# Where the down-projection's gate is applied: on the input matrix ahead of time, or on row sums and two weights inside the stage

## The chip, the cores and the metric

The kernel runs on one core of one Trainium2 chip. The metric is the device time of one execution in microseconds, lower is better; the median of three runs is compared. Engines are called as the profile calls them: PE is the matrix engine (TensorE), DVE the vector engine, ACT the scalar engine, POOL GpSimd, and SP the engine whose queue issues nearly all DMA transfers. SBUF is the on-chip memory, PSUM the accumulators of PE.

## The reference, cut to what matters

One layer of a diffusion backbone on 2048 latent tokens of width 1024, with 256 context tokens in front: RMSNorm and modulation, one input projection for a gated recurrence (HGRN2) and a spatial gating unit, an output projection, then a gated MLP with a 3x3 convolution, and a last RMSNorm. The change concerns only the end:

```python
x = x + g1 * (o @ w_out[l])
h2 = modulate(rmsnorm(x, norm_ffn[l]), sh2, sc2)
x = x + g2 * conv_ffn(h2, w_up[l], conv_w[l], conv_b[l], w_down[l], rows)
return rmsnorm(x, norm_final)
# conv_ffn ends in: return (a * gelu(gc)) @ w_down        (2048 x 2816) @ (2816 x 1024)
```

`g2` is one number for each of the 1024 output columns, computed from the input `c`. Multiplying the product's columns by g2, or the columns of `w_down` by g2 before the product, is the same in exact arithmetic.

## The kernel before

**Precision.** Products are made in three passes on PE: each fp32 operand is split into a high part (a cast on ACT, `split`, line 131) and a low part (a subtraction), and `mm3` adds high x high, high x low and low x high. A split on DVE's `Kept` wrapper shows as line 80.

**Phase one** (the first 1150 us): adaLN vectors, input projection, recurrence and gating units. Work that is not urgent is fed in by a "pump", `bg_q`, which at fixed points of the matmul order lets a generator take one more step. After the blocks that compute the adaLN rows (among them `g_d[1]`, which is g2) come `w_out_ops`, `conv_taps` and `w_down_ops`. The last one loads `w_down` in 22 pieces of 128 x 2 x 512, multiplies each by g2 on DVE (line 970) and stores it to the DRAM tiles `wd_d`.

**The up-projection** (about 1150 to 2019 us) is a fast matrix product with seven products in place of eight; it writes the activations `m_d` to DRAM.

**The down-projection** (2019 us to the end) is one, too. The rows of the result are taken in two halves of 1024, its columns in two halves of 512, and the inner dimension of 2816 in 11 pairs of 128-wide blocks j. There are seven rounds q = 0 to 6. In each round one combination of quarters of the activations is multiplied by one combination of quarters of the weights, for all 11 pairs: 77 steps, n = 11 q + j. A step is 8 row groups x 3 passes = 24 matmuls of 512 columns into the 8 PSUM banks, one bank for each row group i. At the end of a round each bank is emptied (`evict`) and the results go on being added up in the SBUF tiles `odd[i]` and `even[i]` (128 x 2 x 512 each: rows of the second and of the first half, two column halves). What can wait is put in the list `side`, from which one function is taken in each later step (`sums_behind`).

Per step, `load(n + 3)` fetches operands, `prepare(n + 2)` makes the combinations and splits them, and the 24 matmuls of step n follow. In `prepare`, `a` is the activations' operand (into the tile `mhl`), `b` the weights' (into `thl`); both have three buffers. Where a combination is used again it is kept in `sS` and `sT` (`S_`, `T_` for the pair j). Tiles for loads go round: four of `mr` (activations, and rows of x later), five of `wr` inside `sT` (weights). DVE's instructions in this stage are pinned to program order; those of POOL and ACT may be moved by the scheduler that lays out each engine's queue when the kernel is built.

Before the change the rows of x after the first residual (`xn_d`) come in twice: rows of the first half are loaded into `even` in round 0, so that round 1's `evict` adds onto them; rows of the second half are loaded in the steps of round 5 and added in `odd_rows`, two steps later. The last round's results are normed and written out (`odd_sum`, `odd_out`), those of the first half in round 6 (`square`, `root`, `row_out`).

Of the kernel before, what the change touches and what calls it, by code (L numbers as in the profile page):

```python
# [9 lines left out]
F32 = mybir.dt.float32  # L10
# [8 lines left out]
P = 128  # L19
D = 1024  # L20
# [28 lines left out]
def view(t, off, dims):  # L49

    return bass.AP(t.tensor, t.offset + off, [list(t.ap[0])] + [list(d) for d in dims])
# [32 lines left out]
def tile_trunk(ctx, tc, x, c, cx, c_ctx, w_ada, b_ada, norm_mix, norm_ffn, w_in, hg_norm, sgu_g, sgu_b,  # L84
# [30 lines left out]
    xh_d = dr.tile([P, NK, TH], F32, name="xh_d")  # L115
    xl_d = dr.tile([P, NK, TH], F32, name="xl_d")
    wo_d = dr.tile([P, NK, 2, D], F32, name="wo_d")
    wd_d = [dr.tile([P, 2, D], F32, name=f"wd{j}") for j in range(NF // 2)]
    xn_d = [dr.tile([P, D], F32, name=f"xn{i}") for i in range(2 * NCH)]

    def rstd(pool, ss, n, scale, bias=EPS, keep=lambda i: i, out=None):
# [67 lines left out]
    with es1:  # L189
# [16 lines left out]
        def raw_tile():  # L206
            return p1.tile([P, D], F32, tag="raw", name="raw", bufs=3)
# [749 lines left out]
                    st(wo_d[:, k, 1, cl], g)  # L957
                    yield 2.5

        def w_down_ops():  # L960

            for n in range(2):
                cl = slice(n * 512, n * 512 + 512)
                g = pm.tile([P, 512], F32, tag="acc", name="g2")
                ld(g, g_d[1:2, cl].broadcast_to([P, 512]))
                for j in range(NF // 2):
                    raw = raw_tile().rearrange("p (a c) -> p a c", a=2)
                    ld(raw, w_down[2 * j * P:2 * (j + 1) * P, cl].rearrange("(a p) c -> p a c", p=P))
                    yield 9.0
                    pin(V.tensor_mul(raw, raw, view(g, 0, [[0, 2], [1, 512]])))  # L970
                    st(wd_d[j][:, :, cl], raw)
                    yield 2.5

        def silu(dst, scale):
            def f(n0, n, pj):
                t = pm.tile([P, 512], F32, tag="sig", name="sig", bufs=2)
# [4 lines left out]
        def head(hh, h):  # L981

            prev = (hh, h - 1) if h else (hh - 1, NH - 1)
            before = (hh, h - 2) if h > 1 else (hh - 1, NH - 2 + h)
            t = {}

            def pre_v():
                if before[0] >= 0:
                    need(hg_q, (before[0], before[1], "end"))
                    if any(g["key"] == before for g in gates):  # L990
                        gates_done()
                t["sgt"] = ph.tile([P, TH], F32, tag="sgt", name="sgt", bufs=2)
                t["vt"] = ph.tile([P, TH], F32, tag="vt", name="vt", bufs=2)

            def pre_q():
                if prev[0] >= 0:
                    need(hg_q, (prev[0], prev[1], "diag"))
                t["qs"] = ph.tile([P, TH], F32, tag="qs", name="qs")

            def pre_g():  # L1000
                if prev[0] >= 0:
                    need(hg_q, (prev[0], prev[1], "keys"))
                else:
                    need(bg_q, "x1")
                    for e in range(8):
                        bg_q.add(ada_block(e))
                    bg_q.add(w_out_ops())
                    bg_q.add(conv_taps())
                    bg_q.add(w_down_ops())
                t["F"] = pk.tile([P, 2, TH], F32, tag="F", name="F", align_bytes=AL)  # L1010
                t["K"] = pk.tile([P, 2, TH], F32, tag="K", name="K", bufs=2, align_bytes=AL)

            def post():
                hg_q.add(marked(hg(hh, h, t["F"], t["K"], t["qs"], t["vt"], t["sgt"]), (hh, h, "end")))
                if hh == 1:
                    hg_q.add(deferred(h))
            front = tile_banks(4 * HW + h * P, lambda: silu(t["sgt"], 1.0), TH, pre_v)
            front += tile_banks(2 * HW + h * P, lambda: sink_v(t["vt"]))
            front += tile_banks(3 * HW + h * P, lambda: silu(t["qs"], float(P) ** -0.5), TH, pre_q)
            ff = tile_banks(0 * HW + h * P, lambda: sink_gate_x(t["F"], t["K"], 1, 0), TH, pre_g)  # L1020
            fb = tile_banks(1 * HW + h * P, lambda: sink_gate_x(t["F"], t["K"], 0, 1))
            return front, [ff[0], fb[0], ff[1], fb[1]], post
# [464 lines left out]
        return m_d[2 * j + c][:, r * TH:(r + 1) * TH]  # L1487

    def b_src(c, n, j):
        return wd_d[j][:, c, n * 512:(n + 1) * 512]  # L1490

    ops = {}

    def cast(n, a, b, at, bt):

        split(*at, a, V)
        split(*bt, b, V)
        ops[n] = *at, *bt
# [81 lines left out]
    odd = [pd_.tile([P, 2, 512], F32, name=f"odd{i}") for i in range(NCH)]  # L1580
    even = [pd_.tile([P, 2, 512], F32, name=f"even{i}") for i in range(NCH)]
    nf = pd_.tile([P, D], F32, name="nf")
    nw = [0]
    ra, rb = {}, {}

# [11 lines left out]
    def get(t, src):  # L1597
        pin(ld(t, src))
        return t
# [37 lines left out]
    def prepare(n):  # L1637

        if n >= 7 * NJ:
            return  # L1640
        q, j = divmod(n, NJ)
        (a, b), (a2_, b2) = ra.pop(n), rb.pop(n, (None, None))
        if q == 4:
            V.tensor_sub(a, a, a2_)
            V.tensor_sub(b, b, b2)
        cast(n, a, b, slot_s(n), slot_t(n))
        S_, T_ = sS[:, j, :], sTj(j)
        if q == 1:
            V.tensor_add(S_, a2_, S_)
            V.tensor_sub(T_, b2, T_)  # L1650
        elif q == 2:
            V.tensor_sub(S_, S_, a2_)
            V.tensor_sub(T_, b2, T_)
        elif q == 3:
            V.tensor_sub(S_, a2_, S_)
        elif q == 5:
            V.tensor_sub(T_, T_, b2)

    def square(t, ss):
        jk = pd_.tile([P, D], BF16, tag="jk", name="jk")  # L1660
# [2 lines left out]
    def flat(t):  # L1663
        return t.rearrange("p a b -> p (a b)")
# [12 lines left out]

    xts, odd_ss = {}, {}

    def odd_rows(i):  # L1680

        o = odd[i]
        V.tensor_add(flat(o), flat(o), xts.pop(i))
        odd_ss[i] = pd_.tile([P, 2], F32, name=f"oss{i}")
        square(o[:, 1, :], odd_ss[i][:, 1:2])
        V.tensor_scalar(out=odd_ss[i][:, 1:2], in0=odd_ss[i][:, 1:2], scalar1=D * EPS, scalar2=None, op0=ALU.add)
        if i == NCH - 1:
            V.tensor_mul(o[:, 1, :], o[:, 1, :], nf[:, 512:])
# [22 lines left out]
    def sums_behind(q, i):  # L1711
        o, e = odd[i], even[i]
        if q == 1:
            side.append(lambda: V.tensor_add(e[:, 0, :], e[:, 0, :], o[:, 0, :]))
        elif q == 3:
            def f():
                V.tensor_add(e[:, 1, :], e[:, 1, :], o[:, 0, :])
                V.tensor_add(e[:, 1, :], e[:, 1, :], o[:, 1, :])
            side.append(f)
        elif q == 4:  # L1720
            def f():
                V.tensor_add(o[:, 1, :], o[:, 1, :], o[:, 0, :])
                xts[i] = get(mr(), xn_d[NCH + i])
                if i > 1:
                    odd_rows(i - 2)
            side.append(f)
            if i == NCH - 1:
                side.extend([lambda: odd_rows(i - 1), lambda: odd_rows(i)])
        elif q == 5:
            def f():  # L1730
                ss = pd_.tile([P, 2], F32, tag="ss", name="ss", bufs=4)
                square(flat(e), ss[:, 0:1])
                row_out(i, flat(e), root(ss[:, 0:1]))
            side.append(f)

    def evict(q, i, pd):
        o, e = odd[i], even[i]
        if q in (0, 2):
            S.copy(o[:, q // 2, :], pd)
        elif q in (1, 5):  # L1740
            V.tensor_add(e[:, q // 5, :], pd, e[:, q // 5, :])
        elif q in (3, 4):
            V.tensor_add(o[:, 0, :], pd, o[:, 0, :])
        sums_behind(q, i)
# [9 lines left out]
    for n in range(3, 7 * NJ - NB):  # L1754
        q, j = divmod(n, NJ)
        if j == 0:
            pds = banks()
        if n in range(4, 4 + NCH):
            ld(flat(even[n - 4]), xn_d[n - 4])
        if n == 2 * NJ - 3:  # L1760
            ld(nf, norm_final.rearrange("(o d) -> o d", o=1).broadcast_to([P, D]))
            S.mul(nf, nf, float(D) ** 0.5)
        if n == 6 * NJ:
            tail = pd_.tile([P, NJ * TH], F32R, tag="sS", name="tail", align_bytes=AL)
            tail_s = tail[:, :8 * TH].rearrange("p (s w c) -> p s w c", s=4, w=2)
        if q < 6:
            load(n + 3)
            prepare(n + 2)
        else:
            for k in ((2,), (3,), (4,), (5,), (6, 7), (8, 9), (10,))[j]:  # L1770
                prepare(6 * NJ + k)
            for k in ((3,), (4,), (5, 6), (7, 8), (9, 10), (), ())[j]:
                load(6 * NJ + k)
        for i in range(NCH):
            down(pds[i], n, i, j == 0, j == NJ - 1)
            if j == NJ - 1:
                evict(q, i, pds[i])
        for _ in range(1 + (q == 6)):
            if side and j < NJ - 1:
                side.pop(0)()  # L1780
# [29 lines left out]
```

## Time and profile before

| | us |
|---|---|
| runs of the kernel before | 2452.80, 2452.89, 2457.57 |
| their median | 2452.89 |
| the profiled execution | 2449.13 |
| its span on the core | 2447.3 |
| PE busy in it | 2408.3 |
| DVE busy | 1785.5 |
| ACT busy | 943.7 |
| POOL busy | 873.4 |

The granted clock of PE was 0.998 over the profiled execution. In the profile's rows an instruction stands as line, engine, operation, output<-inputs by the program's names, sizes as partitions x elements, and count. In a timeline the first number is the start in us from the span's start and the second the duration; in brackets stands how long the engine was idle before it, and on whom it waited. A row of the windows has the window, its length, then the busy time (and number) of PE, PEld (loading of weights into PE), DVE, ACT and POOL, PE's granted clock, the share of DMA in use and GB/s. A row of waits has who waited on whom, the sum in us, how often, and the longest. A row of a line's or tile's instructions has the shortest, median and longest duration in ns.

### The profile page before, as it was taken

The page shows a single profiled execution, that of the slowest core. Times are in us where ns is not written, and L with a number is a line of the kernel's source. Part 1 is how long each engine was busy: PE and PEld are TensorE (multiplying, and loading weights), DVE is VectorE, ACT ScalarE, POOL GpSimd, SP SyncE. Part 2 cuts the span into 40 slices and gives each one's busy share as a digit, 9 for nine tenths or more (in the row PEclk, how much of TensorE's full clock was granted, in tenths as well). Part 3 has the DMA queues.
Part 4 walks back from the last instruction along what each step waited for, and adds up shares of the span by engine and source line. Part 5 has one row for each costly group of instructions (what it writes and reads, how often), then busy time and mean ns, then how long its engine had stood idle before and what let it go on. Part 6 is the DMA issues. An engine that isn't in the chain of part 4 may idle for free.

```text
span 2447.3 us, 32836 instructions
## 1 busy us (share of the span) xinstructions
PE 2408.3 (98%) x11859; PEld 2000.8 (82%) x11859; DVE 1785.5 (73%) x2445; ACT 943.7 (39%) x1614; POOL 873.4 (36%) x795
## 2 busy tenths in 40 slices
PE   7999999999999999999999999999999999999998
PEld 4788888888888888788788888878888888888887
DVE  5867685756776776466698877769999992776875
ACT  4554334333344433354443333333333342332343
POOL 1232010110111122001688778787778870000002
PEclk9999999999999999999999999999999999999999
DMA  8365446564254234668822222562222238934645
GB/s 310 109 210 171 141 136 209 193 225 147 96 185 155 87 104 149 233 216 261 297 86 88 82 96 83 177 237 85 86 93 94 83 102 349 318 125 146 228 151 197
DMA packets 307855, 400.13 MB, mean 163 GB/s; under 512 B 33113, under 2 KB 216161, under 8 KB 304621
## 3 DMA queue, kind: packets, MB, share of 16 engines
q1 hardware_dynamic: 304404, 397.28, 48.1%
q8 instruction: 94, 1.54, 0.3%
q10 hardware_dynamic: 3289, 0.76, 0.1%
q14 instruction: 68, 0.56, 0.1%
HBM read 288.85 MB, written 109.13 MB: 163 GB/s over the span
## 4 chain that ended last, share of the span: by engine, by line
PE 40%; DVE 7%; issue 3%; POOL 2%; ACT 1%; DMA 0%; SPq 0%; POOLq 0%; ACTq 0%; DVEq 0%
PE up L65 25%; PE dn L65 15%; DVE dn L1377 3%; DVE edges L1382 1%; DVE gp L1458 1%; ACT dn L1374 1%; POOL Al L132 0%; POOL ra L1669 0%; POOL rr L1670 0%; DVE keep L1452 0%; POOL raw L1195 0%; DVE keep L1468 0%; ACT cv L1396 0%; ACT Ah L131 0%; POOL cv L1469 0%
## 5 line engine op out<-in xcount | busy, mean ns | idle before, releaser
L1377 DVE SCALAR_TENSOR_TENSOR dn<-gp,taps,dn 128x1024 f32<-128x1024 f32 x352 | 448.3, 1280 | 21.4 <-ACT dn L1374 18.1
L65 PE MATMUL up<-yf,Ah 128*128 128x512 f32 x1232 | 393.7, 389 | 0.0
L65 PE MATMUL dn<-thl,mhl 128*128 128x512 f32 x1680 | 381.5, 389 | 1.2 <-ACT thl L131 1.2
L132 POOL TENSOR_TENSOR Al<-raw,Ah 128x512 fp32r<-128x512 f32 x264 | 342.9, 1307 | 92.0 <-ACT Ah L131 79.0
L65 PEld LDWEIGHTS dn<-thl,mhl 128*128 128x128 f32 x1680 | 315.0, 188 | 67.7 <-ACT thl L131 2.0
L65 PE MATMUL pj<-xh,whi 128*128 128x512 f32 x896 | 363.1, 406 | 0.0
L65 PE MATMUL pj<-xh,wlo 128*128 128x512 f32 x896 | 350.6, 392 | 2.0 <-DVE wlo L132 2.0
L65 PE MATMUL pj<-xl,whi 128*128 128x512 f32 x896 | 351.4, 392 | 1.1 <-POOL xl L132 1.0
L65 PE MATMUL up<-xah,Al 128*128 128x512 f32 x704 | 275.6, 392 | 3.8 <-POOL Al L132 3.8
L65 PE MATMUL up<-xah,Ah 128*128 128x512 f32 x704 | 274.5, 390 | 0.6 <-ACT Ah L131 0.6
L65 PEld LDWEIGHTS up<-yf,Ah 128*128 128x128 f32 x1232 | 231.2, 188 | 48.1
L131 ACT CAST Ah<-raw 128x512 fp32r<-128x512 f32 x264 | 160.5, 618 | 278.4 <-PE up L65 208.4
L65 PE MATMUL up<-xal,Ah 128*128 128x512 f32 x528 | 205.5, 389 | 0.0
L65 PE MATMUL up<-yf,Al 128*128 128x512 f32 x528 | 205.2, 389 | 0.0
L65 PEld LDWEIGHTS pj<-xh,wlo 128*128 128x128 f32 x896 | 168.3, 188 | 38.2 <-DVE wlo L132 2.7
L65 PEld LDWEIGHTS pj<-xh,whi 128*128 128x128 f32 x896 | 168.6, 188 | 33.3 <-issue 3.5
L65 PEld LDWEIGHTS pj<-xl,whi 128*128 128x128 f32 x896 | 168.8, 188 | 32.2 <-POOL xl L132 1.9
L65 PE MATMUL dn<-wo,o 128*128 128x512 f32 x768 | 182.9, 394 | 2.1 <-ACT o L131 1.6
L580 POOL TENSOR_TENSOR K<-K,tot 128x512 f32<-128x512 f32 x40 | 50.0, 1251 | 343.9 <-PE sc L65 194.5
L65 PEld LDWEIGHTS dn<-wo,o 128*128 128x128 f32 x768 | 141.9, 188 | 31.8 <-ACT o L131 2.0
L65 PEld LDWEIGHTS up<-xah,Al 128*128 128x128 f32 x704 | 132.1, 188 | 36.5 <-POOL Al L132 9.4
L65 PEld LDWEIGHTS up<-xah,Ah 128*128 128x128 f32 x704 | 132.2, 188 | 28.0 <-ACT Ah L131 1.0
(315 smaller groups left out, 3923.7 us busy)
## 6 DMA issues: line engine op xcount, KB each, us to landing
raw<-in_w_up_dram SPq DMA_DIRECT2D x88, 512.0 KB, 4.7
mr<-m SPq DMA_DIRECT2D x85, 512.0 KB, 5.0
raw<-in_w_in_dram SPq DMA_DIRECT2D x68, 512.0 KB, 4.2
sT<-wd SPq DMA_DIRECT2D x88, 256.0 KB, 4.1
raw<-in_w_ada_dram SPq DMA_DIRECT2D x32, 512.0 KB, 3.8
yf<-yd SPq DMA_DIRECT2D x14, 1024.0 KB
m<-cv SPq DMA_DIRECT2D x22, 544.0 KB, 2.7
raw<-in_w_down_dram SPq DMA_DIRECT2D x22, 512.0 KB, 4.3
```

Of the source, the lines that this page charges most:

```text
L65: return self.engine.matmul(out, lhsT, rhs, **kw)
L131: keep(S.copy(hi, raw))
L132: (eng or G).tensor_sub(lo, raw, hi.bitcast(F32))
L580: e.tensor_mul(view(K2, row * W + o, src), view(K, o, src), view(tot, t0, [[4, n], [ts, 2], [0, B]]))
L1374: S.activation(cr, gt[:, 0:RH, 0:GW], AF.Identity, bias=cvb[:, f:f + 1], scale=taps[:, f:f + 1])
L1377: V.scalar_tensor_tensor(out=cr, in0=gt[:, t // 3:t // 3 + RH, t % 3:t % 3 + GW], scalar=taps[:, t * NF + f:t * NF + f + 1], in1=cr, op0=A ...
L1382: V.scalar_tensor_tensor(out=e[:, 0, :], in0=gt[:, 1, t % 3:t % 3 + GW], scalar=taps[:, t * NF + f:t * NF + f + 1], in1=e[:, 0, :], op0=AL ...
L1458: V.tensor_add(g_rows(hh, f + c, n2), quad(p, kind), quad(add, kind))
```

## The change

The gated copy of `w_down` is no longer made: `w_down_ops` and the tiles `wd_d` are removed, and the down-projection loads the same pieces from the input `w_down`. The gate is applied inside the stage, on POOL (`G`):

- In round 5 each prepared weight `b` is multiplied by the second column half of g2 before its cast, and the kept combination `T_`, which round 6 uses, by the first half, after its subtraction. These are 22 multiplications of 128 x 512. The results of rounds 5 and 6 come out gated.
- `even[i]` is multiplied by g2 as a whole behind round 3, and `odd[i]` behind round 4: 16 multiplications of 128 x 1024, run from `side` in the first eight steps of rounds 4 and 5.
- Since the sums are ungated until then, the rows of x are added later, for both halves, in `rows_x`, one step behind the multiplication of `odd[i]`. Both row blocks are loaded in round 5. Round 1's results are copied into `even` by ACT instead of added by DVE; behind round 3 one addition takes the place of two.
- A tile `g2` (128 x 1024) is loaded once at the start of the stage.

```diff
--- before.py
+++ after.py
@@ -115,7 +115,6 @@
     xh_d = dr.tile([P, NK, TH], F32, name="xh_d")
     xl_d = dr.tile([P, NK, TH], F32, name="xl_d")
     wo_d = dr.tile([P, NK, 2, D], F32, name="wo_d")
-    wd_d = [dr.tile([P, 2, D], F32, name=f"wd{j}") for j in range(NF // 2)]
     xn_d = [dr.tile([P, D], F32, name=f"xn{i}") for i in range(2 * NCH)]
 
     def rstd(pool, ss, n, scale, bias=EPS, keep=lambda i: i, out=None):
@@ -957,20 +956,6 @@
                     st(wo_d[:, k, 1, cl], g)
                     yield 2.5
 
-        def w_down_ops():
-
-            for n in range(2):
-                cl = slice(n * 512, n * 512 + 512)
-                g = pm.tile([P, 512], F32, tag="acc", name="g2")
-                ld(g, g_d[1:2, cl].broadcast_to([P, 512]))
-                for j in range(NF // 2):
-                    raw = raw_tile().rearrange("p (a c) -> p a c", a=2)
-                    ld(raw, w_down[2 * j * P:2 * (j + 1) * P, cl].rearrange("(a p) c -> p a c", p=P))
-                    yield 9.0
-                    pin(V.tensor_mul(raw, raw, view(g, 0, [[0, 2], [1, 512]])))
-                    st(wd_d[j][:, :, cl], raw)
-                    yield 2.5
-
         def silu(dst, scale):
             def f(n0, n, pj):
                 t = pm.tile([P, 512], F32, tag="sig", name="sig", bufs=2)
@@ -1006,7 +991,6 @@
                         bg_q.add(ada_block(e))
                     bg_q.add(w_out_ops())
                     bg_q.add(conv_taps())
-                    bg_q.add(w_down_ops())
                 t["F"] = pk.tile([P, 2, TH], F32, tag="F", name="F", align_bytes=AL)
                 t["K"] = pk.tile([P, 2, TH], F32, tag="K", name="K", bufs=2, align_bytes=AL)
 
@@ -1487,7 +1471,7 @@
         return m_d[2 * j + c][:, r * TH:(r + 1) * TH]
 
     def b_src(c, n, j):
-        return wd_d[j][:, c, n * 512:(n + 1) * 512]
+        return w_down[(2 * j + c) * P:(2 * j + c + 1) * P, n * 512:(n + 1) * 512]
 
     ops = {}
 
@@ -1580,6 +1564,8 @@
     odd = [pd_.tile([P, 2, 512], F32, name=f"odd{i}") for i in range(NCH)]
     even = [pd_.tile([P, 2, 512], F32, name=f"even{i}") for i in range(NCH)]
     nf = pd_.tile([P, D], F32, name="nf")
+    g2 = pd_.tile([P, D], F32, name="g2")
+    ld(g2, g_d[1:2, :].broadcast_to([P, D]))
     nw = [0]
     ra, rb = {}, {}
 
@@ -1643,6 +1629,8 @@
         if q == 4:
             V.tensor_sub(a, a, a2_)
             V.tensor_sub(b, b, b2)
+        if q == 5:
+            G.tensor_mul(b, b, g2[:, 512:])
         cast(n, a, b, slot_s(n), slot_t(n))
         S_, T_ = sS[:, j, :], sTj(j)
         if q == 1:
@@ -1655,6 +1643,7 @@
             V.tensor_sub(S_, a2_, S_)
         elif q == 5:
             V.tensor_sub(T_, T_, b2)
+            G.tensor_mul(T_, T_, g2[:, :512])
 
     def square(t, ss):
         jk = pd_.tile([P, D], BF16, tag="jk", name="jk")
@@ -1677,10 +1666,11 @@
 
     xts, odd_ss = {}, {}
 
-    def odd_rows(i):
-
-        o = odd[i]
-        V.tensor_add(flat(o), flat(o), xts.pop(i))
+    def rows_x(i):
+
+        o, (xo, xe) = odd[i], xts.pop(i)
+        V.tensor_add(flat(even[i]), flat(even[i]), xe)
+        V.tensor_add(flat(o), flat(o), xo)
         odd_ss[i] = pd_.tile([P, 2], F32, name=f"oss{i}")
         square(o[:, 1, :], odd_ss[i][:, 1:2])
         V.tensor_scalar(out=odd_ss[i][:, 1:2], in0=odd_ss[i][:, 1:2], scalar1=D * EPS, scalar2=None, op0=ALU.add)
@@ -1714,18 +1704,19 @@
             side.append(lambda: V.tensor_add(e[:, 0, :], e[:, 0, :], o[:, 0, :]))
         elif q == 3:
             def f():
-                V.tensor_add(e[:, 1, :], e[:, 1, :], o[:, 0, :])
-                V.tensor_add(e[:, 1, :], e[:, 1, :], o[:, 1, :])
+                V.tensor_add(e[:, 1, :], o[:, 0, :], o[:, 1, :])
+                G.tensor_mul(flat(e), flat(e), g2)
             side.append(f)
         elif q == 4:
             def f():
                 V.tensor_add(o[:, 1, :], o[:, 1, :], o[:, 0, :])
-                xts[i] = get(mr(), xn_d[NCH + i])
-                if i > 1:
-                    odd_rows(i - 2)
+                G.tensor_mul(flat(o), flat(o), g2)
+                xts[i] = get(mr(), xn_d[NCH + i]), get(mr(), xn_d[i])
+                if i:
+                    rows_x(i - 1)
             side.append(f)
             if i == NCH - 1:
-                side.extend([lambda: odd_rows(i - 1), lambda: odd_rows(i)])
+                side.append(lambda: rows_x(i))
         elif q == 5:
             def f():
                 ss = pd_.tile([P, 2], F32, tag="ss", name="ss", bufs=4)
@@ -1737,8 +1728,10 @@
         o, e = odd[i], even[i]
         if q in (0, 2):
             S.copy(o[:, q // 2, :], pd)
-        elif q in (1, 5):
-            V.tensor_add(e[:, q // 5, :], pd, e[:, q // 5, :])
+        elif q == 1:
+            S.copy(e[:, 0, :], pd)
+        elif q == 5:
+            V.tensor_add(e[:, 1, :], pd, e[:, 1, :])
         elif q in (3, 4):
             V.tensor_add(o[:, 0, :], pd, o[:, 0, :])
         sums_behind(q, i)
@@ -1755,8 +1748,6 @@
         q, j = divmod(n, NJ)
         if j == 0:
             pds = banks()
-        if n in range(4, 4 + NCH):
-            ld(flat(even[n - 4]), xn_d[n - 4])
         if n == 2 * NJ - 3:
             ld(nf, norm_final.rearrange("(o d) -> o d", o=1).broadcast_to([P, D]))
             S.mul(nf, nf, float(D) ** 0.5)
```

## The prediction

> **What bounds the kernel now.** I read the page, the windows, the waits, and last the timeline of each engine in the last stage.
>
> ```profile
> span 2447.3 us, 32836 instructions
> PE 2408.3 (98%) x11859; PEld 2000.8 (82%) x11859; DVE 1785.5 (73%) x2445; ACT 943.7 (39%) x1614; POOL 873.4 (36%) x795
> ```
>
> PE is busy for 98% of the span, so the time changes only where PE is made to wait, or stops waiting. The change touches two places: phase one, where `w_down_ops` runs, and the down-projection at the end.
>
> ```profile
> L970 DVE TENSOR_TENSOR raw<-raw,g x22: 1209/1216/2310, 546.4 to 821.2; 128x1024 f32<-128x1024 f32 x22
> ...
> 546.00:824.00 278.00, 277.95 (x1619) 242.89 (x1618) 192.87 (x274) 107.70 (x223) 36.54 (x37) 1.00 0.43 146
> ...
> PE dn L65 <- ACT thl L131: 1.2, 2, 0.7
> POOL ra L1669 <- ACT jk L1661: 359.2, 3, 357.3
> ```
>
> The first row is the 22 gating multiplications in phase one; the second is the window in which they lie (length, then PE, PEld, DVE, ACT, POOL busy). PE is busy for 277.95 of 278.00 us there. The third row is all that PE waits for in the down-projection between 2036 and 2440 us: 1.2 us. The fourth shows POOL without work there: it stands idle for 357.3 us in one piece.
>
> So PE bounds the down-projection too, and the question is how far ahead of PE the splits of its operands run. A step is one of 77 products (7 rounds q of 11); call the flat number n. ACT casts step n+2 when PE ends step n-1, since three buffers go round:
>
> ```profile
> 2254.93 1.05 ACT L131 CAST mhl<-mr 128x1024 fp32r<-128x1024 f32 x1 [3.87 <-PE dn L65]
> ...
> 2320.17 1.06 ACT L131 CAST mhl<-sS 128x1024 fp32r<-128x1024 f32 x1 [3.82 <-PE dn L65]
> ...
> 2347.37 1.05 ACT L131 CAST mhl<-sS 128x1024 fp32r<-128x1024 f32 x1 [3.20 <-PE dn L65]
> ...
> 2352.81 1.05 ACT L131 CAST mhl<-sS 128x1024 fp32r<-128x1024 f32 x1 [3.25 <-PE dn L65]
> ```
>
> PE starts n=43 at 2254.93 and n=55 (first of round 5) at 2320.17; the step is 2352.81-2347.37 = 5.44 us. VectorE (DVE) in round 4, then its adds at the round's end, then one step of round 5, then the adds that end round 5:
>
> ```profile
> 2266.09 0.68 DVE L80 TENSOR_TENSOR thl<-sT,thl 128x512 fp32r<-128x512 f32 x1
> 2266.69 1.41 DVE L80 TENSOR_TENSOR even<-even,odd 128x512 f32<-128x512 f32 x2
> 2268.02 1.22 DVE L80 TENSOR_TENSOR mr<-mr 128x1024 f32<-128x1024 f32 x1
> 2269.16 0.68 DVE L80 TENSOR_TENSOR sT<-sT 128x512 f32<-128x512 f32 x1
> 2270.44 1.23 DVE L80 TENSOR_TENSOR mhl<-mr,mhl 128x1024 fp32r<-128x1024 f32 x1 [0.59 <-ACT mhl L131]
> ...
> 2318.21 4.87 DVE L80 TENSOR_TENSOR odd<-dn,odd 128x512 f32<-128x512 f32 x8
> ...
> 2324.73 0.68 DVE L80 TENSOR_TENSOR sT<-sT 128x512 f32<-128x512 f32 x1
> ...
> 2349.14 1.21 DVE L80 TENSOR_TENSOR mhl<-sS,mhl 128x1024 fp32r<-128x1024 f32 x1
> 2350.28 0.69 DVE L80 TENSOR_TENSOR thl<-sT,thl 128x512 fp32r<-128x512 f32 x1
> 2350.88 0.68 DVE L80 TENSOR_TENSOR sT<-sT 128x512 f32<-128x512 f32 x1
> 2351.48 0.69 DVE L80 TENSOR_TENSOR odd<-odd 128x512 f32<-128x512 f32 x1
> 2352.08 1.22 DVE L80 TENSOR_TENSOR odd<-odd,mr 128x1024 f32<-128x1024 f32 x1
> 2354.51 0.15 DVE L80 TENSOR_SCALAR oss<-oss 128x1 f32<-128x1 f32 x1 [1.21 <-ACT jk L1661]
> 2354.58 1.22 DVE L80 TENSOR_TENSOR mhl<-sS,mhl 128x1024 fp32r<-128x1024 f32 x1
> ...
> 2377.40 4.87 DVE L80 TENSOR_TENSOR even<-dn,even 128x512 f32<-128x512 f32 x8
> ```
>
> From start to start, an operation on 128x1024 takes DVE 1.14 us (2349.14 to 2350.28) and one on 128x512 takes 0.60. DVE's queue keeps program order, and it is nearly full: in round 5 the step takes 2354.58-2349.14 = 5.44 us, 1.21 of it idle for ACT's square. The weights of n=46 are split at 2266.69; PE starts n=46 at 2254.93+3x5.44 = 2271.25, so the lead in round 4 is 4.5 us. That is all the cover there is.
>
> **The change part by part. Phase one:** 22 multiplications (27 us of DVE by 1.216 each), 22 loads and 22 stores of 512 KB leave, and two broadcasts. PE idles 0.05 us in that window, so this removes nothing from the end: 0, at most 0.05. Reading `w_down` instead of the copy changes an address, not a count or a size: 0.
>
> **Rounds 0 to 3.** Eight loads of x rows move from round 0 to round 5, and one broadcast of g2, 512 KB, is put at the head of SP's queue, with the first loads of the stage behind it.
>
> ```profile
> mr<-m SPq DMA_DIRECT2D x85, 512.0 KB, 5.0
> ...
> L1739 ACT COPY odd<-dn x16: 580/592/648, 2076.6 to 2201.5; 128x512 f32<-128x512 f32 x16
> ```
>
> A load of 512 KB lands 5.0 us after its issue; the ends are -1.2 (all of PE's wait gone) and +5.0 (one landing more in front of everything). I take 0, since loads run three steps, 16 us, ahead of PE. Round 1's eight results are copied by ACT, where DVE added them before; the 16 copies of rounds 0 and 2 are done so already, at 592 ns each under PE's 0.68 per bank (5.44/8): 0.
>
> **What POOL gets.** Eight multiplications of 128x1024 (`e` by g2) in round 4's first eight steps; eight more (`o` by g2) in round 5's first eight; and in each of round 5's eleven prepares two of 128x512 (`b`, `T_`), two steps ahead. Prices, and what POOL and DVE do to each other:
>
> ```profile
> 1598.62 1.28 POOL L132 TENSOR_TENSOR Al<-raw,Ah 128x512 fp32r<-128x512 f32 x1
> 1599.88 1.28 POOL L1469 TENSOR_TENSOR cv<-keep,cv 128x512 f32<-128x512 f32 x1
> ...
> 751.65 1.83 POOL L675 TENSOR_TENSOR nt<-nt,gu 128x512 f32<-128x512 f32 x1 [6.67 <-ACT gu L680]
> ...
> 751.11 1.23 DVE L132 TENSOR_TENSOR wlo<-raw,whi 128x1024 fp32r<-128x1024 f32 x1 [2.43 <-ACT whi L131]
> 752.25 2.31 DVE L970 TENSOR_TENSOR raw<-raw,g 128x1024 f32<-128x1024 f32 x1
> ...
> L1382 DVE SCALAR_TENSOR_TENSOR edges<-gp,taps,edges x66: 270/1076/1392, 1608.8 to 1984.8; 128x64 f32<-128x64 f32 x66
> ...
> L1458 DVE TENSOR_TENSOR gp<-up,keep x88: 675/684/694, 1180.1 to 1977.1; 128x512 f32<-128x512 f32 x88
> ...
> 1220.00:1980.00 760.00, 756.71 (x3328) 623.40 (x3327) 655.53 (x715) 279.41 (x442) 609.69 (x518) 1.00 0.32 107
> ```
>
> POOL does 128x512 every 1.26 us, say 1.25; the trace has no 128x1024 of it, which I take as two halves, 2.5 (an estimate). The rows about 751 us are the heart of this forecast. POOL's multiplication took 1.83 instead of 1.28: it stood until DVE's subtraction was through at about 752.25. DVE's next operation took 2.31 instead of 1.216: POOL's ended at 753.48, and DVE's 1.08 us later. They ran one after the other, not together. The last rows say which operations this hits. POOL is busy for 610 of 760 us there; `edges`, with both inputs in SBUF, is stretched from 270 ns to a median of 1076, while `gp<-up,keep`, which reads one input from PSUM, stays at 675 to 694. In the down-projection every split, add and subtraction of DVE but the adds at a round's end has both inputs in SBUF. So POOL's time must be added to DVE's.
>
> The Trainium skill, SBUF — State Buffer, section Who interferes with whom, states this as an exclusive lock: a DVE instruction with two SBUF inputs and a GpSimd one that reads SBUF never overlap, and issue order decides who stands. The trace agrees (2.31 = 1.23 + 1.08); without the lock the time would be the first rival's. The Trainium skill, GPSIMD Engine Reference, section 3.1, gives 4497 ns for 2048 fp32 columns; halved (an estimate) that is 2.25 for 128x1024 and would lower the sum by 16x0.25 = 4 us.
>
> **Round 4.** DVE per step: two of 1.14, three of 0.60 (the second `even` add is removed) = 4.08; with POOL's 2.5 it is 6.58, 1.14 over the step. Eight such steps: 9.1 less the lead of 4.5 = 4.6 us late at n=54. Then POOL's `b` for n=55 (1.25) and DVE's two splits (1.74) end 2.99 us after PE starts n=54; the step to n=56 is 4.84 (2.34 of DVE, 2.5 of POOL); then the subtraction of `T_` 0.60 and the first add that frees a bank 0.60: 9.03, where PE is through at 5.44. PE waits 3.6 us more; in the trace of before that add began 2 us ahead of it. **Late by 8.2 at n=55.**
>
> **Round 5.** The eight adds read PSUM, so POOL's queue runs beside them for nothing. They end 4.2 us after PE resumes at n=55, the splits of n=57 at 5.9, and PE needs those at 10.9: 4.94 ahead. The next step costs 2.34+0.60 of DVE and 5.0 of POOL = 7.94: 2.44 ahead. Then come seven steps (splits of n=59 to 65) with `rows_x`, which adds both row blocks (2x1.14, one more than before): 2.34+0.60+2.28+5.0 = 10.22, 4.78 over each. 7x4.78-2.44 = 31.0. DVE's wait for ACT's square lies under POOL's work. Splits of n=66: 6.47, 1.0 over. Before round 5's adds DVE splits n=67 (1.74) and does one add (0.60): PE waits 2.3. **Late by 8.2+31.0+1.0+2.3 = 42.5 at n=66.** Behind that POOL has only the small root operations it had, and round 6 runs as before.
>
> **Sum.** The profiled execution took 2449.13 us; 2449.1+42.5 = 2491.6. The median of the runs, 2452.89, lies 3.8 above it; on that scale 2495. Ends: by 1.08, 0.54, 1.23 and 2.46 as what an operation holds (752.25 to the end of the row), the same count gives 35; with the 1.21 us idle of DVE exposed in seven steps it is 51.
>
> **Rivals.** (1) Not slower: no standing for each other in this stage. POOL's 5.0 per step fit in 5.44. DVE's own line in round 5 becomes 2.34+0.60+2.28 and 0.9 to 1.2 of waiting, some 6.2; eight steps use 8x0.76 = 6.1 of the 6.3 us by which n=57 is ahead (2320.17+10.88, less 2324.73 where its splits have ended), and PE waits up to 1 us: 2454. It decides if both engines' operations keep 1.22 and 1.25 us side by side; the rows at 751 us speak against it. (2) POOL's queue order alone, without the standing: the subtraction of `T_`, then 1.25+2.5+1.25 on POOL, a cast of 0.6, two of 0.60: 6.8 and some 0.2 of signals (an estimate), 7.0 per step; 1.56 over in eight, 12.5, less the lead of 6.3, and a little at the rounds' ends: 7 us, 2460. It needs `b` to stand behind `o` in POOL's queue. (3) Worse: ACT's squares, or a queue order that leaves the shared path idle between them, add over 1.5 us to each of 16 steps: 2519. (4) Faster by the relief of phase one: 5 us would be wanted where PE idles 0.05.
>
> **How the numbers follow.** Forecast 0.76, rival 1 0.09, rival 2 0.05, rival 3 0.08, rival 4 0.02. The likeliest gives 2495. Its bounds 35 and 51 are 2488 and 2504; below I also allow that round 4's multiplications find gaps (-8.2) and that rounds' ends cost nothing (-3.3), down to 2476; above some of rival 3, to 2510. Rivals 1, 2 and 4 stay out. A measurement of this kernel tells 0.2%, 4.9 us, from no change: faster 0.02, same 0.09, slower 0.89.
>
> **What would show it.** DVE's 128x1024 operations in rounds 4 and 5 with a mean well over 1.22 us and single ones near 2.3 or 3.6; POOL's of 128x1024 at 2.5 or more; PE waits on `thl`/`mhl` of 40 us in all, none before n=50, most between n=59 and 65 in pieces of 4 to 5 us; phase one with PE as busy as now. I am wrong if the step of round 5 stays under 7 us, or if PE waits elsewhere, for a load of w_down or x.

## The result, and the profile after

The changed kernel takes 2490.08 us (median of four runs, 2488.14 to 2492.80) against 2452.85 for the kernel before (four runs): 37.2 us more, ratio 1.015 with a 95% interval of 1.0132 to 1.0168. The profiled execution took 2490.86 us.

The page of the changed kernel, its span and its engines:

```profile
span 2489.1 us, 32763 instructions
PE 2424.7 (97%) x11859; PEld 2011.4 (81%) x11859; DVE 1809.5 (73%) x2415; ACT 947.1 (38%) x1622; POOL 965.1 (39%) x833
```

The number of matmuls is the same, 11859, so the two traces can be laid side by side matmul by matmul. At the start of round 4 the changed kernel's are 4.7 us late, at the first of round 5 (n=55) 10.8, at n=67 42.0, and nothing is added behind that. From round 4 to the first step of round 6 the change therefore costs 6.1 + 31.2 = 37.3 us; the 4.7 from earlier stages lies within what profiles of kernels with the same earlier stages differ by (below).

The windows of the changed kernel, for the stretch in which the 22 gating multiplications lay in phase one, and for the 100 us around round 5 (columns as in the table's note above: PE, PEld, DVE, ACT, POOL, clock, DMA share, GB/s):

```profile
546.00:824.00 278.00, 277.94 (x1612) 242.61 (x1611) 168.85 (x252) 108.41 (x225) 36.14 (x38) 1.00 0.20 65
2320.00:2420.00 100.00, 78.25 (x293) 60.64 (x291) 93.27 (x82) 27.37 (x46) 65.71 (x30) 0.90 0.47 155
```

In phase one DVE lost 24 us of work and the DMA share fell from 0.43 to 0.20, while PE's busy time went from 277.95 to 277.94: the relief bought nothing. In round 5 the picture is turned over: DVE is busy for 93 of 100 us and PE for 78. What PE waits for in the down-projection, from the waits (the cast of a split is line 130 in this kernel):

```profile
PE dn L65 <- DVE thl L80: 17.7, 9, 3.8
PE dn L65 <- DVE even L80: 4.2, 1, 4.2
PE dn L65 <- ACT thl L130: 1.6, 2, 0.9
```

PE's own timeline shows when:

```profile
2249.63 59.32 PE L65 MATMUL dn<-thl,mhl 128*128 128x512 f32 x261
2309.24 5.78 PE L65 MATMUL dn<-thl,mhl 128*128 128x512 f32 x24 [0.29 <-DVE thl L80]
2315.52 5.52 PE L65 MATMUL dn<-thl,mhl 128*128 128x512 f32 x23 [0.51 <-DVE thl L80]
...
2323.98 34.98 PE L65 MATMUL dn<-thl,mhl 128*128 128x512 f32 x144 [1.59 <-DVE thl L80]
2362.81 7.31 PE L65 MATMUL dn<-thl,mhl 128*128 128x512 f32 x24 [3.84 <-DVE thl L80]
2372.39 7.34 PE L65 MATMUL dn<-thl,mhl 128*128 128x512 f32 x24 [2.27 <-DVE thl L80]
2381.97 7.36 PE L65 MATMUL dn<-thl,mhl 128*128 128x512 f32 x24 [2.23 <-DVE thl L80]
2391.53 5.73 PE L65 MATMUL dn<-thl,mhl 128*128 128x512 f32 x24 [2.21 <-DVE thl L80]
2401.10 8.56 PE L65 MATMUL dn<-thl,mhl 128*128 128x512 f32 x24 [3.84 <-DVE thl L80]
...
2420.32 10.04 PE L65 MATMUL dn<-thl,mhl 128*128 128x512 f32 x36 [4.19 <-DVE even L80]
```

Until 2309 us there is no gap: the lead absorbs the first steps of round 4. Small gaps follow in its last steps, then none for 35 us, and from 2362.81 on PE starts a step each 9.58 us in place of 5.44, behind the split of `thl`. The last row is the wait for round 5's first addition. Now DVE, in two steps of round 4 and in one of round 5:

```profile
2278.28 1.21 DVE L80 TENSOR_TENSOR mr<-mr 128x1024 f32<-128x1024 f32 x1
2279.41 2.88 DVE L80 TENSOR_TENSOR sT<-sT 128x512 f32<-128x512 f32 x1
...
2285.69 2.89 DVE L80 TENSOR_TENSOR sT<-sT 128x512 f32<-128x512 f32 x1
...
2363.88 2.29 DVE L80 TENSOR_TENSOR even<-even,mr 128x1024 f32<-128x1024 f32 x1
2366.09 3.41 DVE L80 TENSOR_TENSOR odd<-odd,mr 128x1024 f32<-128x1024 f32 x1
2370.35 0.15 DVE L80 TENSOR_SCALAR oss<-oss 128x1 f32<-128x1 f32 x1 [0.85 <-ACT jk L1650]
2370.42 1.31 DVE L80 TENSOR_TENSOR mhl<-sS,mhl 128x1024 fp32r<-128x1024 f32 x1
```

and POOL beside them:

```profile
2278.43 3.31 POOL L1708 TENSOR_TENSOR even<-even,g 128x1024 f32<-128x1024 f32 x1 [2.97 <-DVE even L80]
...
2363.43 1.66 POOL L1646 TENSOR_TENSOR sT<-sT,g 128x512 f32<-128x512 f32 x1 [2.37 <-DVE sT L80]
2365.05 3.37 POOL L1713 TENSOR_TENSOR odd<-odd,g 128x1024 f32<-128x1024 f32 x1
2368.38 2.27 POOL L1633 TENSOR_TENSOR sT<-sT,g 128x512 f32<-128x512 f32 x1
```

The pairs are read together. POOL's multiplication of `even` was ready at 2278.43, stood until DVE's subtraction of `mr` was through (about 2279.5), and ended at 2281.74; DVE's next operation, a subtraction of 128x512 that took 0.68 before, took 2.88, and ended 0.55 us after POOL's. In round 5 `odd<-odd,mr` took 3.41 in place of 1.22 around POOL's 128x1024. Each engine's duration holds the other's. The exception is in the groups by shape: the additions that read one operand from PSUM (first row) keep their usual time with POOL at work beside some of them, while those with both operands in SBUF (second row) are stretched on the mean:

```profile
L80 DVE TENSOR_TENSOR odd<-dn,odd 128x512 f32<-128x512 f32 x16 | 9.7, 677 | 0.0
...
L80 DVE TENSOR_TENSOR odd<-odd,mr 128x1024 f32<-128x1024 f32 x8 | 26.1, 3268 | 0.0
```

### The profile page after: what moved, and what is told of

It is laid out like the page before. It is cut to its first block, busy times and chain, and to the rows that moved or that the text cites. A ratio compares the mean times of both kernels' runs of the same rounds, so it can differ in the third digit from the quotient of the medians.

```text
span 2489.1 us, 32763 instructions
## 1 busy us (share of the span) xinstructions
PE 2424.7 (97%) x11859; PEld 2011.4 (81%) x11859; DVE 1809.5 (73%) x2415; ACT 947.1 (38%) x1622; POOL 965.1 (39%) x833
## 4 chain that ended last, share of the span: by engine, by line
PE 37%; DVE 10%; issue 3%; POOL 2%; ACT 1%; DMA 0%; SPq 0%; POOLq 0%; ACTq 0%; DVEq 0%
PE up L65 24%; PE dn L65 12%; DVE dn L1361 3%; DVE odd L80 1%; DVE edges L1366 1%; DVE even L80 1%; DVE mhl L80 1%; DVE gp L1442 1%; ACT dn L1358 1%; DVE thl L80 0%; POOL Al L131 0%; POOL rr L1659 0%; DVE sT L80 0%; POOL ra L1658 0%; DVE keep L1436 0%
## 5 line engine op out<-in xcount | busy, mean ns | idle before, releaser
L65 PE MATMUL dn<-thl,mhl 128*128 128x512 f32 x1680 | 395.6, 398 | 23.6 <-DVE thl L80 17.7
L65 PEld LDWEIGHTS dn<-thl,mhl 128*128 128x128 f32 x1680 | 322.1, 192 | 97.0 <-DVE thl L80 22.0
```

Of the source, the lines that this page charges most:

```text
L65: return self.engine.matmul(out, lhsT, rhs, **kw)
```

## The experiments

The theory: POOL's operations that read SBUF and DVE's with two inputs there run one after the other, so that their times add up in each step. The rivals: POOL's queue order or its place in the chain of dependences; the additional row loads and additions; the earlier stages. Each verdict is against the kernel before, run on the same chip.

**Without the multiplications (no_gate).**

```diff
-        if q == 5:
-            G.tensor_mul(b, b, g2[:, 512:])
...
-            G.tensor_mul(T_, T_, g2[:, :512])
...
-                G.tensor_mul(flat(e), flat(e), g2)
...
-                G.tensor_mul(flat(o), flat(o), g2)
```

> The changed kernel with the four multiplications by g2 on POOL left out, and nothing else: this leaves out the gating of the down-projection. The moved row loads, the added DVE addition per step and round 1's copies on ACT stay. Theory (POOL's operations and DVE's two-input operations on SBUF run one after the other): without POOL's work the round-4 step of DVE is 4.08 us and the round-5 step some 6.2, so the last stage waits at most 1 to 2 us; rounds 4 and 5 lose under 3 of the 37 us, and the ratio to the kernel before is 0.999 to 1.003. The early loss of 5.5 us in phase one and the up-projection, if it comes from another order of the instructions there, is kept (then about +5 us, 1.002); if it is variation from run to run it is not seen in the median. Rival A (the additions of the x rows, their second load or the queue of loads cost the time, not POOL): rounds 4 and 5 still lose over 10 us, ratio 1.005 or more. Rival B (relief of phase one was hidden under the loss): faster than before by more than 5 us.

Measured: 2453.74 us, ratio 0.9996 (0.9986 to 1.0005). All that PE waits for in the down-projection:

```profile
PE dn L65 <- ACT thl L130: 0.7, 1, 0.7
PE dn L65 <- DVE even L80: 0.5, 1, 0.5
```

The additional row loads and additions, the copies on ACT and the missing phase-one work together change nothing that can be measured, in either direction. All of the 37 us hangs on the multiplications by g2.

**POOL writes, and reads nothing (write_only).** For 128x512 two writes, for 128x1024 two and a half:

```diff
-            G.tensor_mul(b, b, g2[:, 512:])
+            for _ in range(2):
+                G.memset(b, 0.01)
...
-                G.tensor_mul(flat(o), flat(o), g2)
+                for _ in range(2):
+                    G.memset(flat(o), 0.01)
+                G.memset(o[:, 0, :], 0.01)
```

> The changed kernel with each multiplication on POOL replaced by writes of a constant to the same tile at the same place in the queue: two writes for 128x512, two and a half for 128x1024, so that POOL is busy about as long (1.1 and 2.3 us, an estimate) and each dependence stays. This leaves out the gating, and the values are a constant; POOL reads nothing from SBUF. Theory (what excludes is POOL's reading of SBUF beside DVE's second read): DVE keeps 1.22 and 0.68 us per operation in rounds 4 and 5, the step of round 5 is 7 us at most (POOL's own queue), and the whole loses 0 to 10 us against the kernel before, ratio 1.000 to 1.005. Rival A (the order of POOL's queue and the chain of dependences through POOL cost the time, whatever POOL does to DVE): 25 to 40 us, ratio 1.010 to 1.016, with DVE's operations at their usual 1.22 and 0.68 but idle behind POOL. Rival B (any POOL operation on SBUF, a write too, keeps DVE out): DVE's operations stretched as in the changed kernel, 30 us or more.

Measured: 2452.48 us, ratio 0.9991 (0.9982 to 1.0000). From its groups by shape, between 2245 and 2440 us:

```profile
L1718 POOL MEMSET odd<- 128x1024 f32 x16 | 15.3, 957 | 0.2
L1648 POOL MEMSET sT<- 128x512 f32 x22 | 11.6, 527 | 17.0 <-DVE sT L80 16.3
L80 DVE TENSOR_TENSOR odd<-odd,mr 128x1024 f32<-128x1024 f32 x8 | 9.7, 1218 | 0.0
```

The same tiles, nearly the same places in POOL's queue (the two writes of `b` came to stand between those of `odd`), some 4.5 us of POOL work in each step (4 x 0.53 and 2.44), and DVE's additions onto `even` and onto `odd` take 1218 ns where they took 2165 and 3268 in the changed kernel. Order and dependences alone cost nothing at this length of POOL's work. For the second rival of the prediction this is a weak test: counted its way, 4.55 us of POOL make a step of 6.55, and 8 x 1.11 less the lead of 6.3 is only 2.6 us (an estimate). What speaks against it is the stretched rows of the changed kernel and its step of 9.58. The Trainium skill, SBUF — State Buffer, section Who interferes with whom, says that DVE's second input collides with a GpSimd instruction that reads SBUF and not with one that only writes it; the run agrees.

**A read of one operand (one_read).** Multiplication by a constant in place of g2:

```diff
-            G.tensor_mul(b, b, g2[:, 512:])
+            G.tensor_scalar(out=b, in0=b, scalar1=0.5, scalar2=None, op0=ALU.mult)
```

and so at the other three places.

> The changed kernel with each multiplication by g2 on POOL replaced by one by a constant (0.5) on the same tile, so that POOL reads one operand from SBUF in place of two; this leaves out the gating by g2. Theory (any POOL operation that reads SBUF and any DVE operation with two inputs there run one after the other): DVE's operations next to it are stretched by what POOL's takes, and the loss follows from the steps: if POOL takes as long as before (2.2 and 1.1 us), the same 35 to 39 us, ratio 1.014 to 1.016; if it takes as little as the writes did (0.95 and 0.53 us), the round-4 step is 5.0, under PE's, and the round-5 step 5.2 + 2.0 = 7.2, seven times 1.8 less some 5 of lead = 8 us and some 2 at the round's end, ratio 1.003 to 1.005; between these by its length. DVE's 128x1024 additions in round 5 have a mean over 1.5 us. Rival (only two operands read by both engines collide): DVE's operations keep 1.22 and 0.68 us, the loss is 0 to 3 us, ratio 1.000 to 1.001.

Measured: 2464.90 us, ratio 1.0045 (1.0031 to 1.0058), and by another way than either side had. Two rows of POOL and four of DVE from its timeline:

```profile
2349.62 2.86 POOL L1713 TENSOR_SCALAR odd<-odd 128x1024 f32<-128x1024 f32 x1
2352.45 1.49 POOL L1633 TENSOR_SCALAR sT<-sT 128x512 f32<-128x512 f32 x1
```
```profile
2349.77 2.05 DVE L80 TENSOR_TENSOR odd<-odd,mr 128x1024 f32<-128x1024 f32 x1
2352.74 1.40 DVE L80 TENSOR_TENSOR mhl<-sS,mhl 128x1024 fp32r<-128x1024 f32 x1
...
2355.87 1.63 DVE L80 TENSOR_TENSOR even<-even,mr 128x1024 f32<-128x1024 f32 x1
...
2360.39 1.40 DVE L80 TENSOR_TENSOR mhl<-sS,mhl 128x1024 fp32r<-128x1024 f32 x1
```

POOL takes longer than for the multiplication by g2 alone (2.86 where 2.2 was held), yet DVE's addition beside it is stretched by 0.83 us only, and it ran wholly inside POOL's 2.86. These two did overlap. Elsewhere in this run a split of 128x1024 kept its 1.21 us (at 2337.83) wholly inside another 2.86 of POOL's. Where DVE is stretched, it is mostly by 0.42 us or twice that: 1.21 becomes 1.63 or 2.05, and 0.68 becomes 1.10 or 1.52. So this form keeps DVE out for about 0.42 us for each 512 columns, and for the rest of its time lets it work; whether the 0.42 us are the part in which POOL reads is not shown. The step is 7.65 us (2352.74 to 2360.39): the 6.2 of the kernel without multiplications and 1.4 of stretching, far from 6.2 plus POOL's own 6. By POOL's length the theory would have had at least the changed kernel's loss; it was 10.8 us. So "one after the other" holds for POOL's operation with two operands in SBUF, as the changed kernel has them, and not for any that reads: the theory was too wide, and the rival, which had no stretching at all, was wrong too. The Trainium skill, SBUF — State Buffer, section Summary: rules for kernel authors, has the second of two such instructions to issue fully blocked until the first finishes; for this form the measurement says otherwise.

**All four on DVE (on_dve).** `G.tensor_mul` becomes `V.tensor_mul` in four places.

> The changed kernel with the four multiplications on DVE in place of POOL, all of the computation done. Theory (both engines' times add up anyway, and DVE's price for the work, 1.14 and 0.60 us, is half of POOL's 2.2 and 1.25): the round-4 step is 4.08 + 1.14 = 5.22 us, under PE's 5.44, so no wait there; the round-5 step is 2.34 + 1.2 + 0.6 + 1.14 + 2.28 and up to 0.9 of waiting for the square on ACT = 7.6 to 8.5, so seven steps lose 2.1 to 3.0 each, 15 to 21, less some 4 of lead and plus up to 4 at the ends of the rounds: 12 to 21 us over the kernel before, ratio 1.005 to 1.009, and faster than the changed kernel by 16 to 25 us. Rival (POOL does take work off DVE, and the time was lost to POOL's order or latency): DVE, with 8 us more per step on it, is slower than the changed kernel or the same, 37 us or more.

Measured: 2487.12 us, ratio 1.0129 (1.0112 to 1.0146): 32.2 over the kernel before, where 12 to 21 were expected. The round-4 step behaved (no gap of PE before the end of the round, where it waited 2.53 us); round 5 took over 10 us a step. DVE and ACT in it:

```profile
2369.39 1.22 DVE L80 TENSOR_TENSOR odd<-odd,mr 128x1024 f32<-128x1024 f32 x1
2374.23 0.15 DVE L80 TENSOR_SCALAR oss<-oss 128x1 f32<-128x1 f32 x1 [3.63 <-ACT jk L1650]
```
```profile
2372.53 1.04 ACT L130 CAST mhl<-sS 128x1024 fp32r<-128x1024 f32 x1 [8.47 <-PE dn L65]
2373.49 0.62 ACT L1650 ACTIVATE jk<-odd 128x512 bf16<-128x512 f32 x1
...
2375.02 0.62 ACT L130 CAST thl<-sT 128x512 fp32r<-128x512 f32 x1 [0.82 <-DVE sT L80]
```

Nothing is stretched; DVE stands. It waits 3.63 us for a square on ACT, which is queued behind a cast that waits for PE to free a buffer. DVE's multiplication of the next `b` stands behind that wait, ACT's cast of `thl` waits for it (last row), and PE waits 2.97 us for this cast. DVE's work had come down, and a circle of waits took its place. That asked for a run of its own.

**The same without that wait (on_dve_late), and the changed kernel without it (pool_late).** The edit is the same in both:

```diff
 def rows_x(i):
-        V.tensor_scalar(out=odd_ss[i][:, 1:2], in0=odd_ss[i][:, 1:2], scalar1=D * EPS, ...)
...
         elif q == 5:
             def f():
+                V.tensor_scalar(out=odd_ss[i][:, 1:2], in0=odd_ss[i][:, 1:2], scalar1=D * EPS, ...)
```

> The four multiplications on DVE, as in the run before, and the small addition to oss (128x1, which waits for the square on ACT) moved out of rows_x into round 6. All of the computation is done. Theory (in the run with everything on DVE it was not DVE's work that cost 11 us a step but its standing for 2.4 to 3.6 us at that addition, behind a square that ACT could only begin after a cast that itself waited for PE): without the standing the step is DVE's 7.56 us, 2.1 over PE's 5.44, seven such steps 15, some 3 of lead off and some 4.5 at the ends of the rounds on: 13 to 20 us over the kernel before, ratio 1.005 to 1.008. Rival (the standing is only where the time shows, and the step is set by the round trip of casts and splits through PE's buffers): 28 us or more, ratio 1.011 or more.

> The changed kernel, multiplications on POOL, with the addition to oss moved into round 6 in the same way. All of the computation is done. Theory (as predicted: DVE's 0.85 us of waiting for the square lies under POOL's multiplication, which would keep DVE out anyway): the step of round 5 stays near 9.6 us and the whole 34 to 39 us over the kernel before, ratio 1.0140 to 1.0160. Rival (that wait is added to the path): seven steps lose 0.85 us less each, 31 us, ratio 1.0127 or under.

Measured, on_dve_late: 2475.46 us, ratio 1.0092 (1.0075 to 1.0109): 22.3 us over the kernel before, 9.9 less than with the wait (32.2) and 14.9 less than the changed kernel (37.2), a little over the 20 expected, which lies within the interval (18.4 to 26.7). pool_late: 2487.95 us, ratio 1.0139 (1.0124 to 1.0155), 34.8 us, within the uncertainty of the changed kernel's 37.2. In the latter's timeline of DVE the standing is gone and the step is what it was:

```profile
2362.00 2.29 DVE L80 TENSOR_TENSOR even<-even,mr 128x1024 f32<-128x1024 f32 x1
2364.21 3.38 DVE L80 TENSOR_TENSOR odd<-odd,mr 128x1024 f32<-128x1024 f32 x1
2367.52 2.32 DVE L80 TENSOR_TENSOR mhl<-sS,mhl 128x1024 fp32r<-128x1024 f32 x1
...
2371.56 2.31 DVE L80 TENSOR_TENSOR even<-even,mr 128x1024 f32<-128x1024 f32 x1
```

2371.56 - 2362.00 = 9.56. The 0.85 us came back at once as a longer split of `mhl` (2.32 for 1.31), since POOL's multiplication of `b` had lain under it. With POOL in the stage the wait is free; with the work on DVE it costs 9.9 us. The windows of on_dve_late over the 24 matmuls of two successive steps show what still held it up:

```profile
2359.75:2367.13 7.38, 7.38 (x24) 5.57 (x24) 7.31 (x9) 0.18 (x1) 0.00 (x0) 0.77 0.53 188
2369.18:2374.92 5.74, 5.74 (x24) 4.42 (x24) 5.67 (x7) 0.19 (x1) 0.00 (x0) 1.00 0.27 96
```

After its wait PE ran the first 24 at a granted clock of 0.77, 1.64 us longer, and ACT's next cast and then DVE wait for PE's end; the step is 9.43 us there and 7.78 in the next. Three such steps make 4.9 us; without them 22.3 would be 17.4 (an estimate).

**Round 4 alone and round 5 alone.** round4_only keeps the multiplication of `even`; round5_only keeps the other three.

> The changed kernel with only the multiplication of even by g2 in round 4 kept on POOL; the gating of b, T_ and odd is left out. Theory (times add up step by step, with the lead in front): eight steps of 6.29 us lose 0.85 each, 6.8, less the lead of 4.5 = 2.3, and up to 3 more at the end of round 4 and in round 5, where DVE has little to spare: 2 to 6 us over the kernel before, ratio 1.001 to 1.0025. Rival (the cost lies in the 128x1024 multiplications as such, eight of the sixteen, and in what they do to the order): half of the whole, 15 us or more, ratio 1.006 or more.

> The changed kernel with the multiplication of even by g2 in round 4 left out, those of b, T_ and odd kept on POOL. Theory: the steps of round 5 keep 9.6 us, and with the 4.5 us of lead whole at their beginning the loss is that of the changed kernel less 4 to 8: 28 to 33 us, ratio 1.0115 to 1.0135. Rival (round 5 is late only because round 4 had eaten the lead and the order of the queues had been upset): 20 us or less, ratio 1.008 or less.

Measured: round4_only 2455.73 us, ratio 1.0012 (1.0002 to 1.0021), 2.6 us; round5_only 2482.76 us, ratio 1.0123 (1.0107 to 1.0139), 29.6 us. PE's timeline in the first, with all of its waits from round 4 on but one of 0.29 us,

```profile
2312.66 5.78 PE L65 MATMUL dn<-thl,mhl 128*128 128x512 f32 x24 [0.51 <-DVE thl L80]
2318.94 65.55 PE L65 MATMUL dn<-thl,mhl 128*128 128x512 f32 x287 [0.50 <-DVE thl L80]
2385.29 38.34 PE L65 MATMUL dn<-thl,mhl 128*128 128x512 f32 x168 [0.80 <-DVE even L80]
```

and in the second:

```profile
2359.94 7.34 PE L65 MATMUL dn<-thl,mhl 128*128 128x512 f32 x24 [3.80 <-DVE thl L80]
2369.52 7.33 PE L65 MATMUL dn<-thl,mhl 128*128 128x512 f32 x24 [2.24 <-DVE thl L80]
```

Eight multiplications of 128x1024 cost 2.6 us in round 4; eight more, with the 22 smaller ones beside them, cost 29.6 in round 5. This fits the room that DVE has in the step, 1.36 us in round 4 and 0.2 (5.44 - 5.22) in round 5; a run with the eight alone in round 5 was not made. The two together, 32.2, fall 5 short of 37.2. That is about the lead of 4.5 us that each run alone may use once, but the difference is no larger than the uncertainty of the three times.

**The kernel before, a second time (before_again).**

> The kernel before once more, for a second profile of it. It is to tell whether PE's start of the up-projection and of the down-projection, 5.5 us later in the changed kernel's profile, lies within what two profiles of one kernel differ by. Theory (variation): matmul by matmul the two profiles of the kernel before differ by several us early on, and the difference of 5.5 is not of the change. Rival (the change reordered something in phase one): the two profiles of the kernel before agree within 1 us up to the down-projection.

Measured: 2455.29 us, ratio 1.0004 (0.9993 to 1.0015). First and last matmul of the down-projection's first steps, for the kernel before in its two profiles and the changed kernel, one fence for each:

```profile
L65 PE MATMUL dn<-Ah,mhl x48: 388/389/389, 2019.1 to 2035.2; 128*128 128x512 f32 x48
```
```profile
L65 PE MATMUL dn<-Ah,mhl x48: 388/389/389, 2022.0 to 2038.1; 128*128 128x512 f32 x48
```
```profile
L65 PE MATMUL dn<-Ah,mhl x48: 388/389/389, 2024.6 to 2040.7; 128*128 128x512 f32 x48
```

Two profiles of one kernel begin the last stage 2.9 us apart, so half of the 5.5 is seen as variation. The changed kernel and its eight variants above, which differ from it in the last stage alone, begin it between 2021.8 and 2027.4 us in their profiles, 5.6 us apart, the lowest of them under the 2022.0 of the kernel before's second profile. So the 5.5 is no sign of the change by itself, and the median of no_gate shows that it doesn't matter.

## Why the prediction was right

**Phase one, 0 us: right.** PE's busy time in that window is unchanged, and no_gate, which has the relief without the cost, isn't faster.

**Rounds 0 to 3, 0 us: right.** The one wait of PE there, 0.7 us in the fourth step, is in the kernel before too; the copies on ACT and the load of g2 are not seen.

**The mechanism: right, with a limit.** DVE's two-input operations and POOL's multiplications ran one after the other in the steps of rounds 4 and 5, and the 37 us went away where POOL only wrote (write_only). The row at 751 us, of two operations in another stage, was enough to foresee it. The prediction did not know that a POOL operation with one operand overlaps with DVE's for most of its time.

**Round 4, late by 8.2 at n=55: it was 6.1.** The step came to 6.29 (2285.69 less 2279.41, up to rounding) and not 6.58, as the multiplication held the path for 6.29 - 4.08 = 2.2 and not 2.5. The gaps began at 2309 us, in n=52, and none came before n=50, as said. PE was 2.5 us later at n=54, where 4.6 were foretold, and 3.6 more at n=55, as foretold.

**Round 5, late by 34.3 more at n=66: it was 29.5** (40.3 - 10.8). The step came to 9.58 and not 10.22. The mis-sized term is the same: POOL's start-to-start times, 1.25 and 2.5, were counted as what it holds, where it held 9.58 - 5.22 = 4.36 in three operations. That is 4 x 1.08 + 0.04, so by the 1.08 that the row at 751 us itself showed. Seven steps make 0.64 x 7 = 4.5. The estimate of 2.25 from the Trainium skill, GPSIMD Engine Reference, section 3.1, was nearer than my 2.5; the trace held 2.2. The other way, the wait at the end of the round was 4.19 where 1.0 + 2.3 were counted: the splits of n=66 ended at 2417.76, 1.6 us after PE's last matmul of the round, and the first addition began behind those of n=67, at 2419.49. With round 4's 2.1 and these 4.5 off and this 0.9 on, 42.5 becomes 36.8; the other 1.2 us to the measured 35.6 are not accounted for.

**The sum, 42.5 at n=66: it was 35.6**, near the bound by held times (35), **and 37.3 at n=67.** The last 1.7 us are a term that the prediction did not have: behind the wait, eight of the 24 matmuls of n=66 ran at half rate, and the step took 7.16 us in place of 5.44. Against the median, 2495 was foretold and 2490.08 came. A part of this nearness is luck: the slow matmuls, which nobody had counted, made up for some of what the sum had too much.

**PE's waits of 40 us: wrong in form.** The rows name 23.5 us. Most of the rest lies in PE's busy time, in groups of 24 matmuls of 7.3 and 8.56 us in place of 5.5 or so, at a lower clock. In the steps before n=65 it is no loss of its own: PE began successive steps 9.58, 9.58, 9.56 and 9.57 us apart whether its 24 matmuls took 7.3 or 5.73, so the path through DVE and POOL set the time. Within n=66 the trace has no further wait, and there the lower clock cost its 1.7 us.

**DVE's wait for the square lies under POOL's work: right** (pool_late, step 9.56). **The rivals:** no standing (2454) and the queue order alone (2460) fall with the stretched rows and the step of 9.58, a worse order (2519) with the step of 9.58, relief of phase one with no_gate.

## What to carry to other kernels

Moving elementwise work to an idle POOL was no relief for DVE here, where both operands of each lie in SBUF: add the two engines' times per step, using what POOL holds, and compare with PE's step. Work put where a step has room and a lead before it is nearly free (2.6 us in round 4), in a full step it is paid in whole, and DVE pays half of what POOL holds for it (1.14 and 0.60 us for 2.2 and 1.08; on_dve_late, 14.9 us under the changed kernel). When work is moved onto a queue in program order, look for an operation on it that waits for another engine behind a wait for PE: a small addition of 0.15 us was worth 9.9 us here. None of the versions that gate inside the stage beats the kernel before, whose gating lies in phase one beside a busy PE for nothing.

## What the runs showed of the hardware that was not expected

- POOL's multiplication of 128x512 or 128x1024 by a constant excludes DVE's two-input operations for a part of its time only, some 0.42 us for each 512 columns: 1.22 us became 2.05, inside POOL's 2.86. The multiplication of two tiles in SBUF kept DVE out for 1.08 us for each 512 columns.
- POOL's writes of a constant (957 ns for 128x1024) leave DVE's additions at 1218 ns.
- After waits of about 2 us PE can run for a while at half its rate: in on_dve_late seven or eight successive matmuls started 427 ns apart where 227 is usual. It came after waits of 1.84 and 2.04 us, and was absent after others of the same 1.84 and 2.04. The Trainium skill, TensorE: Matmul & The Clock Gate, section What's actually happening, describes a gate of half rate with a free-running window of about 3.4 us, after an idle window of that length; eight times 427 ns is 3.4 us, and a window that runs free would explain why equal waits differ, but the waits here were shorter than the page asks for. What sets it off was not tried.
